# Repricing matmuls, scans and running sums in the order planner of a hybrid attention and mLSTM block

## The chip, the cores and the metric

The kernel runs on one core of one Trainium2 chip. The metric is the device time of one execution in microseconds, lower is better. The core has the engines PE (TensorE, matrix multiply), DVE (VectorE), ACT (ScalarE), POOL (GpSimd) and SP (SyncE, which here issues every DMA).

## The reference, cut to what matters

Two layers over 512 latent tokens and 256 context tokens, model width 1024, batch 1, all float32. One layer:

```
h  = rms_norm(x, norm_g) * (1 + scale) + shift          # scale, shift, gate = silu(c) @ w_mod + b_mod
aq,ak,av,az, bq,bk,bv,bo,bz,bg, cq,ck,cv,cz, gm = split(h @ w_in)
y_a = rms_norm(softmax_1 @ v - lam * softmax_2 @ v) * silu(az)      # A: 4 heads, 2-D rotary
y_b = sigmoid(bo) * rms_norm(mlstm forward + mlstm backward) * silu(bz)   # B: 4 heads, gates bg
y_c = neighbourhood_attention(cq, ck, cv, bias) * silu(cz)          # C: 8 heads
x   = x + gate * ((sum_n sigmoid(gm_n) * (y_n @ w_br_n)) @ w_out)
```

The last layer gives no context output; a final rms_norm ends the program. B's gate values are turned into prefix sums and prefix maxima along the 768 tokens before its heads can begin.

## The kernel before, in words

The work of a layer comes in stages: branch C, with B's gates worked out beside it (`branch_b_gates`), then branch A, branch B, the merge (`merge`: gate projections `gm` and branch projections, three rounds) and the output projection with the norm that leads to the next layer (`finish`). The long projections (`proj`, `proj_v`, tile `pj` in PSUM) are the main stream of PE. Each float32 product is three passes (high part by high part, high by low, low by high) over 128x128 weights with 512 or 256 moving columns; the split weights are the tile `wh`, whose low part is mostly made on POOL.

Heads run beside the main stream as generators. A head of C or A makes scores on PE (tile `gp`, a ring of three PSUM banks, or `sc`, one buffer), takes a row minimum on DVE, an exponential on ACT, normalises on DVE, transposes on PE and multiplies by the values on PE. B does the same with `tensor_tensor_reduce` (a product or sum with a running sum or minimum along the row) in the place of the softmax. `mod_rows` makes the modulation of later stages during the first layer's merge with 112 more instructions of that kind on tiles of 128x512. In the profile they stand as CUSTOM_DVE_ANT_0, followed by a DVE_READ_ACCUMULATOR2_ANT.

**The order is written by a planner.** While the program is built, the class `Sched` keeps a clock for each engine (T["P"] for PE, T["D"] for DVE and so on). Each instruction passes through `Sched.run` with a price in ns; it starts at the later of its engine's clock and the end of what it depends on plus a latency (LAT: 200 after PE, 130 after DVE, 150 after ACT). At every three or six matmuls of the main stream, `slot` looks at the side generators. One whose next step is to use PE goes on when its inputs are ready by PE's planned clock; one whose next step is on another engine may be 400 ns early (EARLY). Side work also pauses when DVE or ACT is planned more than 4000 ns ahead of PE (BACK), for `mod_rows` 1200 ns (REST). So the prices decide how many projection matmuls stand between a score and the transposes that need its softmax. The chip then runs each engine's list in the order written; the prices appear in no instruction.

Prices of DVE, ACT and POOL work are in `Timed.__getattr__` (all such instructions carry L345 in the profile, DMA issues L332), those of matmuls in `mm` (L381); transposes (L385) cost 109 ns. In `branch_b_gates` stand the only three scans of a layer (L1408, L1410, L1417), on 112x768:

```
V.tensor_tensor_scan(ib[:, ::-1], xf[:, ::-1], mk0[:, ::-1], 0.0, ALU.add, ALU.mult)
V.tensor_tensor_scan(pb, xf, mk1, 0.0, ALU.add, ALU.mult)
V.tensor_tensor_scan(mx, aa, aa, ib[:, 0:1], ALU.max, ALU.max)
```

Their generator runs beside the scores of the first head pair of C (`c_pair`). The row minimum of such a score is the tile `m` in the profile, its exponential writes `p` and gives the bank of `gp` back.

Of the kernel before, what the change touches and what calls it, by code (L numbers as in the profile page):

```python
# [12 lines left out]
F32 = mybir.dt.float32  # L13
# [284 lines left out]
def _space(ap):  # L298
    return getattr(ap, "space", None)


def _elems(ap):
    n = 1
    for s in list(ap.shape)[1:]:
        n *= int(s)
    return n


class Timed:
# [5 lines left out]
    def __getattr__(self, name):  # L315
        f = getattr(self.real, name)

        def call(*args, **kw):
            aps = [v for v in list(args) + list(kw.values()) if hasattr(v, "shape")]
            n = max(_elems(v) for v in aps)  # L320
            small = sum(1 for v in aps if _elems(v) == 1 and n > 1)
            psum = any(_space(v) == PSUM for v in aps[1:] + aps[:1])
            writes = [kw["out"] if "out" in kw else args[0]]
            if "accum_out" in kw:
                writes.append(kw["accum_out"])
            if name == "tensor_tensor_reduce":
                writes.append(args[-1])
            reads = [v for v in aps if not any(v is w for w in writes)]
            if name == "dma_start":
                out = kw["out"]  # L330
                self.sched.dma(int(out.shape[0]), int(out.shape[0]) * _elems(out) * 4, reads, writes)
                return f(*args, **kw)  # L332
            if self.eng == "D":
                one = len([v for v in aps if _elems(v) == n]) <= 2 and name in ("tensor_copy", "tensor_scalar", "memset")
                cost = n / (1.92 if one and not psum else 0.96) + 69.0 + 61.0 * small
                if name == "reciprocal":
                    cost = 69.0 + 8.0 * n
                if name == "tensor_tensor_reduce":
                    cost += 220.0
            elif self.eng == "A":  # L340
                cost = n * 0.8333 + (51.0 if psum else 93.0) + 93.0 * small
            else:
                cost = n * 2.15 + 130.0
            self.sched.run(self.eng, cost, reads, writes)
            return f(*args, **kw)  # L345
        return call
# [3 lines left out]
def kernel(ctx: ExitStack, tc: tile.TileContext, a: dict, out: bass.AP):  # L350
# [15 lines left out]
    S_ = Sched(bufs)  # L366
# [10 lines left out]

    def mm(o, l, r, start, stop, cost=None):
        n = _elems(o)
        S_.run("P", cost or (max(107.0, 0.4167 * n) + 2.0 if l.dtype != F32 else 1.67 * max(n, 128)), [l, r], [o])  # L380
        PE.matmul(o, l, r, start=start, stop=stop)  # L381

    def tr(o, i, idn):
# [197 lines left out]
    def mod_end(l, j, ps):  # L581

        yield from acq("t")
        rows = ring("t", [T])
        ACT.copy(out=rows[:, 0:512], in_=ps)
        rel("pj")
        yield "P"
        yield from acq("gp", "P")
        pt = ring("gp", [512])
        for b in range(4):  # L590
            mm(pt[:, 2 * b:2 * b + 2], rows[:, 128 * b:128 * b + 128], csel, True, True, 250.0)
        rel("t")
        yield
        pv = pt[:, 0:8].rearrange("p (b s) -> p b s", s=2)
        dst = modc[l][:, 4 * j:4 * j + 4, :]
        V.tensor_tensor(dst, pv,
                        prm[l][:, PRM_BMOD + 4 * j:PRM_BMOD + 4 * j + 4].unsqueeze(2).to_broadcast([128, 4, 2]), ALU.add)
        rel("gp")
        if j in (2, 3):
            k0 = 4 * (j - 2)  # L600
            V.scalar_tensor_tensor(gsc[l][:, k0:k0 + 4], dst, 1.0,
                                   prm[l][:, PRM_NG + k0:PRM_NG + k0 + 4].unsqueeze(2).to_broadcast([128, 4, 2]),
                                   ALU.add, ALU.mult)
        hit(modf[l][j])
# [70 lines left out]
    def mod_start():  # L675

        tags = ("pt", "pt", "v", "v", "pt", "pt")
        for u, (j, q) in enumerate(units):
            if q == 0:
                S_.need("pj")  # L680
                ps = ring("pj", [512])
            w = first_w[u]
            S_.until(lambda: S_.ready("P", [w], []) <= S_.T["P"])
            for i in range(2):
                k = 2 * q + i
                g = 32 * (k % 4)
                mm(ps[g:g + 32, :], cfz[:, k, :], w[:, 512 * i:512 * i + 512], k < 4, k >= 4, 430.0)
                S_.slot()
            if q == 3:
                S_.urgent(mod_end(0, j, ps))  # L690
            if u % 3 == 2 or u == 15:
                S_.free[tags[u // 3]].append(S_.T["P"] + S_.LAT["P"])
                if u in (2, 5):
                    fetch("pt", range(12, 15) if u == 2 else range(15, 16))
                    W.early = u == 2
        S_.free["cb"].append(S_.T["P"] + S_.LAT["P"])
# [31 lines left out]
    def norm_rows(acc, n, dg, aflag, res, nflag, tags):  # L728

        nt = n // 128  # L730
        yield from wait(aflag, KD, "P")
        ms, r = small(NT, "ms"), small(NT, "rr")
        for t0 in range(0, nt, 4):
            m = min(4, nt - t0)
            yield from acq("gp", "P")
            p = ring("gp", [512])
            for b in range(m):
                tr(p[:, 128 * b:128 * b + 128], acc[:, 128 * (t0 + b):128 * (t0 + b) + 128], ident)
            yield
            V.tensor_reduce(ms[:, t0:t0 + m], p[:, :128 * m].rearrange("p (b d) -> p b d", d=128), axis=AX.X, op=ALU.add)  # L740
            rel("gp")
        V.tensor_scalar(ms[:, :nt], ms[:, :nt], 1.0 / D, EPS, ALU.mult, ALU.add)
        yield from rsqrt_cols(r[:, :nt], ms[:, :nt], nt, "rt")
        for b in range(nt):
            V.tensor_scalar(dg[:, 128 * b:128 * b + 128], ident, r[:, b:b + 1], None, ALU.mult)
        for o in range(0, n, 512):
            w = min(512, n - o)
            yield from acq("gp", "P")
            p = ring("gp", [512])
            mm(p[:, :w], ones, dg[:, o:o + w], True, True)  # L750
            res.append(p[:, :w])
        hit(nflag)
        for t in tags:
            rel(t)
# [1159 lines left out]
```

## Time and profile before

| | |
|---|---|
| median of 3 runs | 1908.1 us (1907.88 to 1908.18) |
| the profiled execution's own time | 1906.09 us |
| its span, first to last instruction | 1904.3 us |
| PE busy | 1820.7 us, 96% |
| DVE busy | 1340.0 us, 70% |
| ACT busy | 858.7 us, 45% |
| POOL busy | 644.6 us, 34% |
| mean granted TensorE clock | 0.986 of full speed |

Busy time of PE is modelled from overlapping instructions, so it is the idle time and the start to start intervals that tell more. The profiled execution is 2.0 us below the median of the three runs and 1.8 us longer than its span.

### The profile page before, as it was taken

What the parts mean: (1) busy time and instruction counts of PE and PEld (TensorE: products, weight loads), DVE (VectorE), ACT (ScalarE), POOL (GpSimd) and SP (SyncE); (2) the same over time, 40 slices, a digit from 0 to 9 for tenths busy, and PEclk for the clock granted to TensorE, in tenths of its full rate; (3) what the DMA queues carried; (4) which work ended last, traced back from release to release, by engine and by line L of the source; (5) the groups of instructions that cost most, each with busy time, mean ns of one, the idle gap of its engine ahead of it and who ended that gap; (6) DMA issues with size and microseconds to landing.
All of it is one profiled execution on the core that took longest, in us unless ns stands there. A gap on an engine that the chain in (4) does not pass through costs nothing. (4 is left out here: it accounts for less than half of the span.)

```text
span 1904.3 us, 31909 instructions
## 1 busy us (share of the span) xinstructions
PE 1820.7 (96%) x11140; PEld 1604.8 (84%) x11140; DVE 1340.0 (70%) x3168; ACT 858.7 (45%) x1932; POOL 644.6 (34%) x563
## 2 busy tenths in 40 slices
PE   5999999999999999999999889999999999999996
PEld 2989998988899888888888779898888888788886
DVE  6676767888888775777763887766887787722336
ACT  4455555554555453222233444644555454432343
POOL 1332322221223322333335443432212323344455
PEclk9999999999999999999999989999999999999998
DMA  8333322222342453665546434333222424544444
GB/s 324 95 100 97 114 83 83 64 78 64 104 120 80 119 160 124 217 198 199 191 154 212 114 99 125 106 95 97 75 67 72 136 87 147 152 154 161 158 163 128
DMA packets 148479, 243.56 MB, mean 128 GB/s; under 512 B 18400, under 2 KB 52544, under 8 KB 148320
## 3 DMA queue, kind: packets, MB, share of 16 engines
q1 hardware_dynamic: 148320, 241.53, 40.5%
q8 instruction: 88, 1.44, 0.3%
q14 instruction: 71, 0.58, 0.1%
HBM read 199.45 MB, written 27.33 MB: 119 GB/s over the span
## 5 line engine op out<-in xcount | busy, mean ns | idle before, releaser
L381 PE MATMUL pj<-h,wh 128*128 128x512 f32 (+1 forms) x5664 | 1123.1, 352 | 2.7 <-ACT h L345 1.8
L381 PEld LDWEIGHTS pj<-h,wh 128*128 128x128 f32 x5664 | 900.9, 191 | 126.6 <-ACT h L345 2.0
L345 POOL TENSOR_TENSOR wh<-wr,wh 128x512 fp32r<-128x512 f32 (+1 forms) x409 | 563.7, 1385 | 1120.1 <-ACT wh L345 1066.3
L345 ACT CAST wh<-wr 128x512 fp32r<-128x512 f32 (+1 forms) x416 | 256.4, 621 | 385.5 <-PE pj L381 217.7
L381 PE MATMUL pj<-wh,h 128*128 128x256 f32 (+1 forms) x1728 | 236.2, 288 | 5.6 <-DVE h L345 3.7
L381 PEld LDWEIGHTS pj<-wh,h 128*128 128x128 f32 x1728 | 217.9, 191 | 9.2 <-DVE h L345 6.0
L345 DVE TENSOR_TENSOR pt<-gp,pt 128x512 fp32r<-128x512 f32 (+1 forms) x224 | 123.9, 573 | 87.8 <-ACT pt L345 86.5
L345 ACT CAST pt<-gp 128x512 fp32r<-128x512 f32 (+1 forms) x224 | 105.5, 496 | 152.1 <-PE gp L385 151.5
L381 PE MATMUL pj<-v,wh 128*128 128x512 f32 (+1 forms) x576 | 160.5, 358 | 0.0
L385 PE MATMUL gp<-ident,p 128*128 128x128 f32 x720 | 110.5, 276 | 17.6 <-DVE p L345 12.2
L381 PE MATMUL gp<-pt,v 128*128 128x256 f32 x864 | 117.2, 283 | 0.1
L381 PEld LDWEIGHTS pj<-v,wh 128*128 128x128 f32 x576 | 103.3, 189 | 15.7
L385 PEld LDWEIGHTS gp<-ident,p 128*128 128x128 f32 x720 | 84.1, 141 | 36.2 <-issue 17.9
L381 PEld LDWEIGHTS gp<-pt,v 128*128 128x128 f32 x864 | 110.5, 190 | 2.3 <-DVE pt L345 0.3
L345 ACT ACTIVATE t<-pj 128x512 f32<-128x512 f32 (+1 forms) x118 | 63.4, 537 | 102.4 <-PE pj L381 102.3
L381 PE MATMUL pj<-qk,wh 128*128 128x512 f32 (+1 forms) x288 | 103.1, 358 | 0.5 <-DVE qk L345 0.5
L345 DVE SCALAR_TENSOR_TENSOR t<-t,pj 128x512 f32<-128x512 f32 x66 | 38.4, 594 | 77.6 <-PE pj L381 77.6
L381 PE MATMUL sc<-qk 128*128 128x512 f32 (+1 forms) x360 | 83.1, 339 | 6.4 <-ACT p L345 4.8
L345 DVE TENSOR_REDUCE mna<-sc 128x1 f32<-128x768 f32 (+1 forms) x80 | 67.7, 846 | 30.3 <-PE sc L381 29.9
L345 ACT ACTIVATE p<-sc,mna 128x768 f32<-128x768 f32 (+1 forms) x80 | 65.5, 819 | 46.8 <-DVE mna L345 46.5
L345 DVE CUSTOM_DVE_ANT_0 sc<-cb,dt 128x512 f32<-128x512 f32 x56 | 56.6, 1011 | 36.2 <-DMA cb<-in_wmodr_dram 35.1
L345 DVE CUSTOM_DVE_ANT_0 sc<-cb,prm 128x512 f32<-128x512 f32 x56 | 62.6, 1118 | 25.3 <-DMA cb<-in_wmodr_dram 24.0
(145 smaller groups left out, 2089.8 us busy)
## 6 DMA issues: line engine op xcount, KB each, us to landing
wr<-in_wu_dram SPq DMA_DIRECT2D x296, 256.0 KB, 2.9
cb<-in_wmodr_dram SPq DMA_DIRECT2D x64, 256.0 KB, 3.8
wr<-in_wout_dram SPq DMA_DIRECT2D x64, 256.0 KB, 2.9
p<-afd SPq DMA_DIRECT2D x80, 192.0 KB, 4.1
wr<-in_wbr_dram SPq DMA_DIRECT2D x48, 256.0 KB, 2.9
q<-qk SPq DMA_DIRECT2D x160, 64.0 KB, 2.2
cb<-vd SPq DMA_DIRECT2D x32, 256.0 KB, 3.3
qk<-in_xT_dram SPq DMA_DIRECT2D x16, 384.0 KB, 6.3
```

The lines of the kernel that those rows point to most:

```text
L345: return f(*args, **kw)
L381: PE.matmul(o, l, r, start=start, stop=stop)
L385: PE.transpose(o, i, idn)
```

## The change

Three prices of the planner are altered; no operation is added or removed.

```
                 if name == "reciprocal":
                     cost = 69.0 + 8.0 * n
-                if name == "tensor_tensor_reduce":
-                    cost += 220.0
+                if name == "tensor_tensor_scan":
+                    cost = n / 0.48 + 430.0
...
-        S_.run("P", cost or (max(107.0, 0.4167 * n) + 2.0 if l.dtype != F32 else 1.67 * max(n, 128)), [l, r], [o])
+        S_.run("P", cost or (max(95.0, 0.4167 * n) + 13.5 if l.dtype != F32 else 1.67 * max(n, 128)), [l, r], [o])
```

A matmul of 512 columns goes from 215.3 to 226.9 ns, one of 256 from 109.0 to 120.2 ns. A scan of 768 goes from 869 (the third one, with a scalar operand, 930) to 2030 ns. A running sum goes down by 220 ns: in `mod_rows` from 944 to 724, in `c_pair` from 678 to 458 ns.

## Rows read from the trace of the kernel before

**Rows 1.** The page: busy us (share of the span) and instructions of each engine.

```profile
PE 1820.7 (96%) x11140; PEld 1604.8 (84%) x11140; DVE 1340.0 (70%) x3168; ACT 858.7 (45%) x1932; POOL 644.6 (34%) x563
```

**Rows 2.** Busy us by stretch: branches, first merge, branches; then granted clock, DMA.

```profile
150.00:750.00 600.00, 593.22 (x3940) 537.35 (x3939) 464.08 (x1281) 309.81 (x774) 161.58 (x168) 1.00 0.33 99
750.00:1050.00 300.00, 299.89 (x1680) 261.72 (x1679) 203.09 (x358) 87.48 (x157) 119.42 (x81) 1.00 0.58 193
1150.00:1700.00 550.00, 531.03 (x3262) 466.23 (x3263) 404.20 (x996) 274.22 (x643) 176.77 (x166) 0.99 0.36 106
```

**Rows 3.** Waits of PE, whole span: us in total, times, longest us.

```profile
PE gp L385 <- DVE p L345: 12.2, 12, 2.4
...
PE sc L381 <- ACT p L345: 4.8, 8, 1.6
```

**Rows 4.** Timeline of PE, first layer: start us, us, [idle before <-releaser].

```profile
91.84 0.40 PE L381 MATMUL gp<-qk 128*128 128x256 f32 x2
...
95.35 1.57 PE L381 MATMUL pj<-h,wh 128*128 128x512 f32 x9
99.73 0.80 PE L381 MATMUL gp<-qk 128*128 128x256 f32 x2 [2.81 <-ACT p L345]
```

**Rows 5.** Timeline of PE, second layer.

```profile
1121.80 0.40 PE L381 MATMUL gp<-qk 128*128 128x256 f32 x2
...
1125.68 1.58 PE L381 MATMUL pj<-h,wh 128*128 128x256 f32 x9
1134.16 0.79 PE L381 MATMUL gp<-qk 128*128 128x256 f32 x2 [6.91 <-ACT p L345]
```

**Rows 6.** Busy us by stretch (order of Rows 2), stretches of low granted clock.

```profile
99.10:105.90 6.80, 6.17 (x26) 5.77 (x27) 6.11 (x21) 4.62 (x13) 1.61 (x2) 0.50 0.28 68
1130.00:1140.20 10.20, 6.04 (x16) 4.98 (x17) 9.52 (x22) 4.40 (x11) 1.49 (x2) 0.50 0.32 92
```

**Rows 7.** Timeline of DVE: first layer's two sum scans, second layer's last scan.

```profile
86.45 3.41 DVE L345 TENSOR_TENSOR_SCAN pt<-pt,t 112x768 f32<-112x768 f32 x2
...
1129.03 1.82 DVE L345 TENSOR_TENSOR_SCAN v<-v,pt 112x768 f32<-112x768 f32 x1
...
1132.45 0.42 DVE L345 TENSOR_REDUCE m<-gp 128x1 f32<-128x256 f32 x1
```

**Rows 8.** Timeline of ACT, second layer.

```profile
1133.54 0.47 ACT L345 ACTIVATE p<-gp,m 128x256 f32<-128x256 f32 x1 [8.20 <-DVE m L345]
```

**Rows 9.** Timeline of PE: 512 columns back to back, and 256 columns.

```profile
1395.14 1.59 PE L381 MATMUL gp<-pt,v 128*128 128x256 f32 x12
1396.57 0.62 PE L381 MATMUL pj<-h,wh 128*128 128x512 f32 x2
...
1751.69 11.26 PE L381 MATMUL pj<-h,wh 128*128 128x512 f32 x48
1762.78 0.39 PE L381 MATMUL pj<-v,wh 128*128 128x512 f32 x1
```

**Rows 10.** Timeline of DVE and POOL in the first merge: running sums.

```profile
817.57 0.76 DVE L345 CUSTOM_DVE_ANT_0 sc<-cb,prm 128x512 f32<-128x512 f32 x1
817.91 3.27 POOL L345 TENSOR_TENSOR wh<-wr,wh 128x512 fp32r<-128x512 f32 x2 [6.41 <-ACT wh L345]
...
820.13 1.60 DVE L345 CUSTOM_DVE_ANT_0 sc<-cb,prm 128x512 f32<-128x512 f32 x1
821.66 0.14 DVE L345 DVE_READ_ACCUMULATOR2_ANT dt<- 128x1 f32 x1
```

**Rows 11.** Groups by shape, whole span: xcount, busy us, mean ns, idle before.

```profile
L345 DVE CUSTOM_DVE_ANT_0 sc<-cb,prm 128x512 f32<-128x512 f32 x56 | 62.6, 1118 | 25.3 <-DMA cb<-in_wmodr_dram 24.0
L345 DVE TENSOR_REDUCE mna<-sc 128x1 f32<-128x768 f32 x64 | 61.0, 953 | 23.0 <-PE sc L381 22.6
...
L345 DVE SCALAR_TENSOR_TENSOR p<-p,sma 128x768 f32<-128x768 f32 x32 | 38.9, 1217 | 1.1
...
L345 DVE CUSTOM_DVE_ANT_0 p<-gp,cb,m 128x256 f32<-128x256 f32 x64 | 31.0, 484 | 9.3
```

## The prediction, made before the change was run

> **What bounds the kernel now.** I read the page first. PE is busy for 96% of the span and no other engine for more than 70% [rows 1], so PE's list sets the end, and a new order can win or lose only what PE does not spend on streaming. The windows by stage say where that is: in the first merge PE idles 300 - 299.89 = 0.11 us, in the branch stages 6.78 us in the first layer and 18.97 us in the second, together 25.75 us [rows 2]. The list of PE's waits names what it waits for there, mostly transposes behind a softmax and scores behind an exponential that holds their PSUM buffer [rows 3]. The largest single wait of a branch, 6.9 us, is a score. The timelines find it and a smaller brother at the same place of each layer, beside B's gates: 2.81 us at 96.9 [rows 4] and 6.91 us at 1127.3 [rows 5]. The idle time is not all they cost: with each comes a stretch in which the granted clock is 0.50 of full speed, 1.2 instead of 2.4 GHz, 6.8 us in the first layer and 10.2 in the second [rows 6].
>
> **Why PE waits there.** The waiting score needs a bank of gp; the bank comes back with an exponential, which waited 8.20 us for the row minimum on DVE [rows 8]. That minimum, at 1132.45, stands in DVE's list behind the three scans and their neighbours [rows 7]. A sum scan takes 1.7 us in the first layer (3.41 for two) and the maximum scan 1.82 in the second [rows 7]; the planner counted 0.87 and 0.93. So the planner believed that DVE was free earlier than it is, and put too few matmuls ahead of the score.
>
> **The change, part by part.** No instruction changes its work; all effects are of order. The sum is made against the profiled execution (1906.09 us, 1.8 outside its span) and carried to the median, which is 2.0 us higher.
>
> Scans. The three go up by 1161, 1161 and 1100 ns, 3.42 us in all; by those rows about 2.6 were missing. All three lie ahead of the minimum in question, so planned PE has 3.42 us more to fill before the score that waits. Against this, the matmuls between the first score of the pair and the blocked one fill more planned time. They run for 95.35 + 1.57 - 91.84 = 5.1 us in the first layer [rows 4] and 5.5 in the second [rows 5]; at 6.6%, the mean rise of the price (below), that is 0.34 and 0.36 us. The softmax's own running minimum, 220 ns cheaper, takes off as much again. Net 2.85 us more real cover in either layer (3.42 - 0.35 - 0.22). The first wait, 2.81, goes, and I let its low clock go with it: half of 6.8 is 3.4, so 6.2 us. The second falls to 6.91 - 2.85 = 4.06, which is longer than the 2.81 that already came with a low clock, so I leave that in place: 2.8 us. Gain 9.0. Bounds: nothing, if the generators fall differently and the minimum stays behind everything else; and both waits with both low stretches, 2.81 + 3.4 + 6.91 + 3.0 = 16.1 (of the second stretch 1130.0 to 1140.2 only the 6.0 us after 1134.2 ran work, half of it lost).
>
> Matmuls. The 48 of 512 columns that start at 1751.69 end their turn at 1762.78: 231 ns each; the 12 of 256 from 1395.14 to 1396.57: 119 ns [rows 9]. The new prices, 226.9 and 120.2, are right to 2%; the old ones were 7 and 8% short. Being right is no gain in itself. PE's own work is the same; a price that was short put 5 to 10% more matmuls between a score and its dependents than the plan needed, a hidden reserve against DVE work that is also priced short. The reduce of 768 takes 953 ns against 930 counted, but the scaled difference after it 1217 against 930 [rows 11]. That reserve now goes. A softmax chain of A is 953 + 1217 and an exponential and a scaling between, an estimate of 4 us with hand-overs from those rows; the price rises by 5.4% at 512 columns and 10.3% at 256, and 6.6% over the mixture (an estimate from equal numbers of both by time, rounded down because transposes keep theirs), which is 0.26 us of cover. The two commonest waits of PE stand there 12 and 8 times [rows 3]. If each of the 20 grew by 0.26, 5.2 us; if as many again opened, 10.4. If one wait shields the next, as PE that stands still gives every other chain time, close to nothing. I take 3 us, rather more than half of the first, because chains overlap; bounds 0 and 10.4.
>
> Running sums. Where POOL does nothing, 512 columns take 0.76 us plus 0.14 to read the sum; beside POOL's subtraction of weights the same instruction takes 1.60 [rows 10]; the mean of the first half of them is 1118 ns [rows 11]. The plan had 944 and gets 724, so this edit moves away from the rows. In C, 484 ns plus a read stand against 678 before and 458 after, about as far off on the other side. In C and B it cuts 0.2 us more cover off a chain; I charge 1 us, between nothing and 20 x 0.22 = 4.4. In the merge I charge nothing: PE waits 0.11 us there [rows 2], and DVE has 300 - 203 = 97 us free, 24 of them spent ahead of the first half of these sums, waiting for the DMA that feeds them [rows 11]. What it costs without that cover is a rival below.
>
> The Trainium skill, page "SBUF — State Buffer", section "Who interferes with whom", says that DVE work with two SBUF inputs and GpSimd work that reads SBUF exclude each other for a whole instruction. The jump from 0.76 to 1.60 us agrees with it. By that rule the honest price of a running sum is about 850 ns alone and over 1.6 us beside POOL, never 724, and the sum would carry the second rival's charge instead of nothing.
>
> Sum: -9.0 + 3 + 1 = -5.0 us: 1901.1 for such an execution as the profiled one, 1903.1 against the median.
>
> **The rivals.** *The reserve eats the gain.* The scan waits shrink, but waits behind DVE grow by 6 to 12 us. For it: DVE is priced short in most chains; against it: 20 waits are few among thousands of matmuls. At 8 us lost, 1907, no change.
>
> *The reserve costs more than the scans give* (slower). Same place, branches A and B of the second layer, where DVE is fullest and 19 of the 25.75 us of idling lie [rows 2]. It decides when more is lost than the 9.0 us won and 3.8 besides: all of both upper bounds, 10.4 + 4.4 = 14.8, gives 1908.1 - 9.0 + 14.8 = 1913.9, and one new stretch of low clock like that of the first layer, 3.4 us, 1917.
>
> *Running sums jam the merge* (slower). Planned 24.6 us too fast in all (112 x 0.22), mod_rows is spread over less of the merge; DVE's list then holds a sum that waits for its DMA ahead of the operation that frees a projection bank. Two banks of 24 x 231 ns, 11 us, cover it; beyond that PE stands. At worst 13.6 us: 1908 - 5 + 13.6 = 1917. Against it: the 0.11 us of now.
>
> *The new price of scans does not reach the spot.* If the order around the gates stays as it is, only the charges are left: 1908 to 1912.
>
> **How the numbers follow.** Forecast, clearly faster, 46%: 1903.1, own range 1893 to 1904.2. Reserve eats the gain 23%; reserve wins 16%; running sums jam the merge 9%; scans miss the spot 6%, of which I give 4 to no change and 2 to slower. About 0.2%, 3.8 us, is what a measurement of this kernel can tell from no change. So faster 46%, same 27%, slower 27%. The range reaches down to 1893, where nearly all of the 16.1 us would come in, and up to 1916, which takes in all but the worst of the slower cases.
>
> **What would show it.** Right: the waits of 2.81 and 6.91 us on ACT p at the scores beside the gates fall under 0.5 and to about 4, DVE's list has the minimum m nearer to or ahead of the scans, and the low clock near 100 us is gone. Matmul intervals stay at 231 and 119. The charge would show as idle time in the two branch windows, 25.75 us now: up to 30 or so fits the sum, 35 and more means the reserve was worth more than I think, and under 25 that it was worth nothing. Idle time in the first merge above 1 us would show the running sums at work. Wrong altogether: new low-clock stretches in the branches, each of which takes about 3.4 us, at places that no term here names.

## The result and the profile after

| | before | after |
|---|---|---|
| median of 4 runs beside each other | 1907.99 us (1907.79 to 1908.18) | 1937.39 us (1933.77 to 1941.16) |
| profiled execution, its span | 1906.09, 1904.3 us | 1933.77, 1932.0 us |
| mean granted TensorE clock | 0.986 | 0.988 |

The changed kernel is slower: 1.0157 times the time before, interval 1.0145 to 1.017, 29.4 us by the medians and 27.7 by the two spans. That is outside the forecast's range (1893 to 1916), on its upper side.

The page, busy time by engine (beside [rows 1]):

```profile
PE 1829.1 (95%) x11140; PEld 1602.8 (83%) x11140; DVE 1336.6 (69%) x3165; ACT 859.1 (44%) x1932; POOL 640.5 (33%) x566
```

PE runs the same 11140 instructions and the clock is no lower, so no work was added and the clock gate did not take the time. The windows by stage say where PE stands still (order of [rows 2]: busy us of PE, PEld, DVE, ACT, POOL, then granted clock, DMA share, GB/s):

```profile
150.00:750.00 600.00, 581.76 (x3849) 522.64 (x3849) 460.25 (x1268) 304.66 (x763) 155.35 (x160) 1.00 0.32 96
750.00:1050.00 300.00, 297.19 (x1647) 257.99 (x1646) 188.52 (x344) 83.51 (x150) 106.11 (x75) 1.00 0.56 187
1150.00:1700.00 550.00, 522.49 (x3216) 455.84 (x3215) 421.81 (x1037) 277.64 (x656) 176.21 (x166) 0.99 0.35 104
```

PE idles 18.24 us in the first branch window instead of 6.78, 2.81 in the merge instead of 0.11, and 27.51 in the second branch window instead of 18.97: 22.7 us more in the three. Over the whole span idle time grows by 19.3 us and "busy" by 8.4 for the same instructions; busy time is modelled, so idle time does not show the whole loss. The windows are also fixed in time. The changed kernel reaches the second layer's gates some 24 us later, so that its second branch window holds 6.7 us of waits at the gates, which stood before 1150 us in the kernel before. A table further down counts idle time between the same matmuls instead. PE's waits over the whole span name the partners (total us, times, longest; beside [rows 3]):

```profile
PE gp L385 <- DVE p L345: 11.4, 15, 1.7
...
PE gp L385 <- DVE o L345: 10.4, 10, 3.1
PE gp L385 <- ACT p L345: 7.3, 3, 4.4
PE sc L381 <- ACT p L345: 6.6, 9, 1.6
PE sc L381 <- DVE den L345: 6.0, 7, 1.8
...
PE pj L381 <- DVE t L345: 2.8, 4, 0.9
```

Of the two waits that I had counted, one shrank (12.2 to 11.4) and one grew (4.8 to 6.6). Most of the new time lies where little or nothing stood before: transposes that wait for a finished head `o` of B, and scores that wait for B's `den`, had these rows in the kernel before:

```profile
PE sc L381 <- DVE den L345: 1.1, 3, 0.5
...
PE gp L385 <- DVE o L345: 0.8, 2, 0.5
```

The two places that the scans were to mend, in PE's timeline of the changed kernel (beside [rows 4] and [rows 5]):

```profile
96.79 2.30 PE L381 MATMUL pj<-h,wh 128*128 128x256 f32 x18
103.52 0.64 PE L385 MATMUL gp<-ident,pt 112*128 112x112 f32 x2 [4.43 <-ACT p L345]
...
1149.19 4.38 PE L381 MATMUL pj<-h,wh 128*128 128x256 f32 x24
1156.30 0.50 PE L381 MATMUL gp<-qk 128*128 128x256 f32 x2 [2.73 <-ACT p L345]
...
1170.19 0.66 PE L385 MATMUL gp<-ident,p 128*128 128x128 f32 x4 [1.78 <-ACT p L345]
```

and DVE's timeline ahead of the minima `m` that they hang on:

```profile
97.35 4.55 DVE L345 COPY pt<-v 48x768 f32<-48x768 f32 x7
101.82 0.41 DVE L345 TENSOR_REDUCE m<-gp 128x1 f32<-128x256 f32 x1
...
1152.61 2.08 DVE L345 TENSOR_TENSOR_SCAN v<-v,pt 112x768 f32<-112x768 f32 x1
1154.61 0.39 DVE L345 TENSOR_REDUCE m<-gp 128x1 f32<-128x256 f32 x1
```

In the second layer the minimum moved up right behind the scan and the wait fell from 6.91 to 2.73 us, but waits of 1.06 and 1.78 us for `p` and two shorter ones for `pt` follow it, which makes 6.7 us again. In the first layer it now stands behind seven copies, 4.55 us of DVE work that is no scan; the wait grew from 2.81 to 4.43 and sits at the gate transposes. The low clock shrank at the first place (3.4 us at 103.3 instead of 6.8 at 99.1); behind the second, 6.8 us remain of 10.2. In branch B of the second layer a stretch of 3.4 us is new, at the end of a wait of 3.10 us for `o`; one of 6.8 us at 1379.1 of the kernel before, in branch A, has no counterpart there (first three lines: after; last: before):

```profile
103.30:106.70 3.40, 3.18 (x9) 2.50 (x10) 3.09 (x12) 3.40 (x15) 2.16 (x3) 0.51 0.00 0
1171.70:1178.50 6.80, 5.79 (x25) 5.19 (x26) 6.55 (x18) 1.39 (x3) 3.04 (x3) 0.50 0.27 77
1574.50:1577.90 3.40, 2.85 (x9) 2.47 (x10) 2.95 (x10) 0.89 (x5) 0.00 (x0) 0.50 0.34 117
...
1379.10:1385.90 6.80, 5.92 (x16) 4.75 (x17) 3.89 (x15) 2.08 (x5) 0.00 (x0) 0.50 0.15 39
```

Matmuls run at the old intervals: 20 of 512 columns take 1755.46 - 1750.84 = 4.62 us, 231 ns each, as in [rows 9]:

```profile
1750.84 4.79 PE L381 MATMUL pj<-h,wh 128*128 128x512 f32 x20
1755.46 0.39 PE L381 MATMUL pj<-v,wh 128*128 128x512 f32 x1
```

### The profile page after: what moved, and what is told of

It is laid out like the page before. It is cut to its first block, busy times and chain, and to the rows that moved or that the text cites. A ratio compares the mean times of both kernels' runs of the same rounds, so it can differ in the third digit from the quotient of the medians.

```text
span 1932.0 us, 31924 instructions
## 1 busy us (share of the span) xinstructions
PE 1829.1 (95%) x11140; PEld 1602.8 (83%) x11140; DVE 1336.6 (69%) x3165; ACT 859.1 (44%) x1932; POOL 640.5 (33%) x566
## 4 chain that ended last, share of the span: by engine, by line
PE 62%; DVE 24%; DMA 5%; issue 4%; ACT 3%; POOL 1%; SPq 1%; DVEq 0%; ACTq 0%; POOLq 0%
PE pj L381 48%; PE gp L381 7%; DVE p L345 5%; PE gp L385 4%; DMA cb<-in_wmodr_dram 3%; PE sc L381 3%; DVE qk L345 3%; DVE t L345 3%; DVE sc L345 2%; DVE pt L345 2%; DVE ht L345 1%; DMA p<-afd 1%; DVE mna L345 1%; ACT p L345 1%; DVE h L345 1%
## 5 line engine op out<-in xcount | busy, mean ns | idle before, releaser
L381 PE MATMUL pj<-h,wh 128*128 128x512 f32 (+1 forms) x5664 | 1115.0, 351 | 4.9 <-ACT h L345 2.2
L381 PEld LDWEIGHTS pj<-h,wh 128*128 128x128 f32 x5664 | 900.0, 190 | 130.3 <-ACT h L345 2.6
L381 PE MATMUL pj<-wh,h 128*128 128x256 f32 (+1 forms) x1728 | 243.5, 291 | 5.6 <-DVE h L345 2.7
L381 PEld LDWEIGHTS pj<-wh,h 128*128 128x128 f32 x1728 | 222.7, 194 | 9.2 <-DVE h L345 4.4
L381 PE MATMUL pj<-v,wh 128*128 128x512 f32 (+1 forms) x576 | 160.1, 358 | 1.2 <-DVE t L345 1.2
L385 PE MATMUL gp<-ident,p 128*128 128x128 f32 x720 | 110.3, 277 | 18.6 <-DVE p L345 11.4
L381 PEld LDWEIGHTS pj<-v,wh 128*128 128x128 f32 x576 | 103.3, 189 | 18.1 <-DVE t L345 2.3
L381 PE MATMUL gp<-pt,v 128*128 128x256 f32 x864 | 117.2, 283 | 0.6 <-DVE pt L345 0.6
L385 PEld LDWEIGHTS gp<-ident,p 128*128 128x128 f32 x720 | 82.5, 141 | 39.7 <-issue 13.8
L381 PEld LDWEIGHTS gp<-pt,v 128*128 128x128 f32 x864 | 110.6, 190 | 2.8 <-DVE pt L345 0.8
L381 PE MATMUL pj<-qk,wh 128*128 128x512 f32 (+1 forms) x288 | 103.1, 358 | 0.4 <-DVE qk L345 0.4
L381 PE MATMUL sc<-qk 128*128 128x512 f32 (+1 forms) x360 | 83.8, 341 | 13.1 <-ACT p L345 6.6
L381 PEld LDWEIGHTS sc<-qk 128*128 128x128 f32 x360 | 57.3, 188 | 29.6 <-ACT p L345 12.6
L345 POOL TENSOR_TENSOR cb<-mskc,t 128x256 f32<-128x256 bf16 x64 | 51.5, 837 | 68.9 <-PE gp L381 35.7
```

The lines of the kernel that those rows point to most:

```text
L385: PE.transpose(o, i, idn)
```

## The experiments

Every kernel is the one before with the lines shown, so all differ in the written order alone; each was timed beside the kernel before on the same chip. "+20" means the difference of the two medians. Three theories were put to the test. *The reserve*: the old short matmul price and the long price of running sums gave DVE cover, and the change took it away. *Running sums*: they alone do the harm, by the merge. *The order*: the old order was a lucky one, and any other order loses some 20 us.

### The three parts alone and in pairs

Matmul price alone (m_only):

```
-        S_.run("P", cost or (max(107.0, 0.4167 * n) + 2.0 if ...
+        S_.run("P", cost or (max(95.0, 0.4167 * n) + 13.5 if ...
```

> Only the matmul price is new; scans and running sums keep the old prices. Theory 1 (the short matmul price was a reserve that covered DVE work which is also priced short): 15 to 30 us slower than before, with more idle time of PE in the branch stages. Theory 2 (the cheaper running sums cost the time): within 4 us of before. Theory 3 (the order of before is a lucky draw, any new order is slower by about the same): 15 to 30 us slower, like every other kernel here.

Scan price alone (s_only):

```
+                if name == "tensor_tensor_scan":
+                    cost = n / 0.48 + 430.0
```

> Only the price of the scans is new. Theories 1 and 2: 3 to 9 us faster than before, with the 6.91 us wait of the second layer's gates down to about 4 and nothing else touched, as six instructions are priced anew. Theory 3: 10 to 30 us slower, since the orders part at the first layer's gates and never meet again.

Running sums alone (r_only):

```
-                if name == "tensor_tensor_reduce":
-                    cost += 220.0
```

> Only the price of the running sums is new. Theory 1: within 5 us of before. Theory 2: 15 to 30 us slower, with waits of PE for DVE in the first merge and in branch B. Theory 3: 10 to 30 us slower, without such a place.

Pairs: matmuls and scans (m_s), scans and running sums (s_r), matmuls and running sums (m_r), the edits above put together.

> Matmul and scan prices new, running sums as before. Theory 1: 10 to 25 us slower, that is nearly all of the change, less the 3 to 9 us that the scans give. Theory 2: 0 to 9 us faster. Theory 3: 15 to 30 us slower.

> Scan and running sum prices new, matmuls as before. Theory 1: within 8 us of before. Theory 2: 10 to 25 us slower. Theory 3: 10 to 30 us slower.

> Matmul and running sum prices new, scans as before. Theory 1: 20 to 35 us slower, more than the whole change. Theory 2: 15 to 30 us slower, as the running sums alone. Theory 3: 15 to 30 us slower.

| kernel | median us | ratio to before, interval | difference |
|---|---|---|---|
| m_only | 1926.83 | 1.0106, 1.0086 to 1.0125 | +19.3 |
| s_only | 1900.64 | 0.996, 0.9946 to 0.9974 | -6.9 |
| r_only | 1920.47 | 1.0067, 1.0052 to 1.0082 | +12.9 |
| m_s | 1930.39 | 1.012, 1.0105 to 1.0135 | +22.8 |
| s_r | 1910.90 | 1.002, 1.0011 to 1.003 | +3.2 |
| m_r | 1949.22 | 1.0216, 1.0201 to 1.0231 | +41.5 |
| all three | 1937.39 | 1.0157, 1.0145 to 1.017 | +29.4 |

The single differences add up to 25.3, near the 29.4 of the whole. They are not independent: the matmul price costs 19.3 alone and 26 to 30 beside the others (22.8 + 6.9, 41.5 - 12.9, 29.4 - 3.2); the running sums cost 6.6 to 22.2 by what stands beside them (29.4 - 22.8, 41.5 - 19.3); the scans give 6.9 to 12.1 except beside the matmuls alone, where they cost 3.5. Two parts do harm, each by itself.

The scan price alone gives about as much as the forecast said of it. PE's timeline at the gates of s_only, both layers (L383 and L387 are L381 and L385 of before), and its windows:

```profile
108.92 0.50 PE L383 MATMUL gp<-qk 128*128 128x256 f32 x2 [0.82 <-ACT p L347]
...
1132.10 0.50 PE L383 MATMUL gp<-qk 128*128 128x256 f32 x2 [1.35 <-ACT p L347]
...
1136.96 0.50 PE L383 MATMUL gp<-qk 128*128 128x256 f32 x2 [1.55 <-ACT p L347]
...
1148.88 1.11 PE L387 MATMUL gp<-ident,p 128*128 128x128 f32 x4 [6.58 <-DVE pt L347]
```

```profile
85.00:150.00 65.00, 61.92 (x437) 56.71 (x436) 53.60 (x129) 30.12 (x78) 23.13 (x21) 1.00 0.37 106
...
150.00:750.00 600.00, 594.84 (x3950) 539.38 (x3949) 458.14 (x1286) 312.41 (x781) 165.18 (x170) 1.00 0.33 99
...
1150.00:1700.00 550.00, 533.80 (x3270) 471.11 (x3270) 398.83 (x999) 274.33 (x638) 177.62 (x166) 0.99 0.35 104
```

In the first layer the score that waited 2.81 us has no wait now (a later one has 0.82), and the granted clock is 1.00 where it was 0.95. Idle time there did not shrink, 3.08 us instead of 2.81, since a wait of 1.90 us for `pt` came in: what is gained is the clock. In the second layer the 6.91 became 1.35 and 1.55, but a new wait of 6.58 us behind them comes with a low clock of its own: transposes of `p` need a bank of `gp` that DVE empties into `pt`, in its list behind copies for the gates. The line of the kernel before for the first window:

```profile
85.00:150.00 65.00, 62.19 (x431) 58.17 (x431) 50.32 (x134) 29.81 (x79) 23.23 (x19) 0.95 0.37 104
```

Idle time of the two branch windows is 5.16 + 16.20 = 21.4 us.

The matmul price alone makes PE idle 20.79 + 24.67 = 45.5 us there (the whole change 45.75), of which 6.9 are the second layer's gate wait, late enough to fall into the window. It brings the `o` row, and at the first layer's gates a wait that was 2.81 us is 6.34:

```profile
150.00:750.00 600.00, 579.21 (x3837) 520.95 (x3835) 462.82 (x1259) 305.10 (x758) 153.58 (x158) 1.00 0.32 95
...
1150.00:1700.00 550.00, 525.33 (x3258) 460.85 (x3257) 424.29 (x1044) 279.97 (x660) 178.05 (x168) 0.99 0.35 106
```

```profile
PE gp L385 <- DVE o L345: 10.6, 12, 1.9
...
103.42 0.64 PE L385 MATMUL gp<-ident,pt 112*128 112x112 f32 x2 [6.34 <-ACT p L345]
```

What such a wait is made of is seen in the changed kernel, timelines of DVE, PE and POOL in the second layer's branch B:

```profile
1571.53 0.15 DVE L345 SCALAR_TENSOR_TENSOR hs<-ht,hs 128x2 f32<-128x2 f32 x1
1571.71 1.18 DVE L345 TENSOR_TENSOR ht<-hs 128x2 f32<-128x2 f32 x1
1572.92 1.23 DVE L345 SCALAR_TENSOR_TENSOR ht<-ht,hm 128x2 f32<-128x2 f32 x1
...
1574.38 0.61 DVE L345 TENSOR_SCALAR o<-gp,hs 128x128 f32<-128x128 f32 x2
...
1575.05 1.11 PE L385 MATMUL gp<-ident,o 128*128 128x128 f32 x4 [3.10 <-DVE o L345]
...
1571.60 2.54 POOL L345 TENSOR_TENSOR wh<-wr,wh 128x512 fp32r<-128x512 f32 x2 [1.01 <-ACT wh L345]
```

Two steps on 128x2 numbers take 1.2 us each while POOL subtracts weights and 0.15 when it does not, as the running sums of [rows 10] do. No price of the planner knows of that; here PE waits it out.

The running sums alone lose most clearly in a place that I had not named. In r_only PE idles 5 us near 360, in branch A, and the granted clock goes to 0.75. No running sum stands in DVE's list between 352 and 367 us, so their price must have acted there through the order of other work; how is not known:

```profile
355.00:365.00 10.00, 5.04 (x24) 3.17 (x22) 8.61 (x22) 5.00 (x15) 3.12 (x3) 0.75 0.40 108
```

In r_only's first merge PE idles 0.00 us (300 - 300.00), so there the merge theory falls. In the whole change the jam that it describes does occur, small (2.8 us in 4 waits, above). But m_only, with the old price of running sums, has it too (the first line below), while r_only and s_r have no such wait, so it needs the matmul price. Beside that price and 7% on DVE (below) the running sums do bring it back: none in m_s_dve107, 3.8 us in all_dve107. PE's waits in m_only, then PE's timeline and DVE's in the changed kernel:

```profile
PE pj L381 <- DVE t L345: 3.9, 3, 2.3
...
860.35 0.39 PE L381 MATMUL pj<-v,wh 128*128 128x256 f32 x1 [0.91 <-DVE t L345]
...
858.08 0.76 DVE L345 CUSTOM_DVE_ANT_0 sc<-cb,prm 128x512 f32<-128x512 f32 x1 [0.97 <-DMA cb<-in_wmodr_dram]
...
859.61 0.68 DVE L345 SCALAR_TENSOR_TENSOR t<-t,pj 128x512 f32<-128x512 f32 x1
```

A running sum waits 0.97 us for its DMA ahead of the operation that frees a bank of `pj`.

### Is it any new order, or a constant cover?

A matmul price 0.5 ns higher than before (nudge), and a constant cover of 300 ns on the whole change (all_margin300); MARGIN is the planner's own setting, 0 until now:

```
# nudge
-        ... (max(107.0, 0.4167 * n) + 2.0 if ...
+        ... (max(107.0, 0.4167 * n) + 2.5 if ...
# all_margin300: the whole change and
-    MARGIN = 0.0
+    MARGIN = 300.0
```

> The kernel before with each matmul counted half a nanosecond dearer (2.0 becomes 2.5 ns in its price, 0.2 to 0.5%), nothing else. It alters no price in a way that matters and is there to draw another order. Theory 1 and 2: within 4 us of before. Theory 3: 10 to 30 us slower.

> The whole change, and the planner's margin (the time that a side step on PE has to be ready ahead of PE's clock, so far 0) set to 300 ns: the reserve that the matmul price gave up is given back as a constant. Theory 1: at least half of the 29 us comes back, 0 to 15 us slower than before. Theory 2: the waits of the merge stay, but those of branch B shrink: 10 to 25 us slower. Theory 3: 15 to 30 us slower.

nudge: 1907.97 us, 0.9999 (0.999 to 1.0009), though 2862 of PE's 11140 instructions, counted in order, are not the ones that stand at the same place before. A different order costs nothing by itself, as far as one such order tells. all_margin300: 1932.90 us, 1.0128 (1.0113 to 1.0143), about 5 us better than the whole change: 0.3 us ahead of every step, more than the 0.26 of which I thought, does not bring the loss of the whole change back. With the matmul price alone a constant was not tried.

### DVE dearer by a factor

If it is the ratio of the two prices that counts, DVE should go up as matmuls did (5.4% and 10.3%). One line behind the DVE prices, in five kernels with the matmul price and one without it:

```
+                cost *= 1.07     # m_dve107: matmul price
+                cost *= 1.07     # m_s_dve107: matmul and scan price
+                cost *= 1.07     # all_dve107: whole change
+                cost *= 1.09     # all_dve109: whole change
+                cost *= 1.26     # all_dve126: whole change
+                cost *= 1.15     # s_dve115: scan price, old matmul price
```

> Only the matmul price new, and every price of DVE 1.07 times as high, so that the two engines stand to each other as before; ACT, POOL and all latencies stay. Ratio theory (what costs is how dear DVE is counted against PE, because DVE's list is dense and the shortfall adds up along a stage; a constant margin per step can't mend it): at least two thirds of the 20 us of the matmul price come back, within 7 us of before. Chain theory (each chain lost a constant piece of cover, and the margin of 300 ns was aimed at the wrong steps): 10 to 18 us slower than before, as 1.07 on DVE adds only some 0.2 us to a chain.

> The whole change, and every price of DVE 1.09 times as high; by the sums of the plan's own prices DVE then stands to PE nearly as it did before the change. Ratio theory: 0 to 8 us faster than before, as the price of the scans still helps. Chain theory: 15 to 25 us slower than before.

> The whole change, and every price of DVE 1.26 times as high, which brings the sum of its prices close to DVE's busy time in the trace, 1337 us against 1301. Ratio theory: the best of all, 5 to 20 us faster than before. Chain theory: 5 to 15 us slower than before. A third way it could go, if a plan that counts DVE too dear starts side work too late and the main stream runs out of buffers: slower than the one with 1.09.

> Only the scan price new, and every price of DVE 1.15 times as high, with the old matmul and running sum prices: more reserve than the kernel before has. Ratio theory: 10 to 20 us faster than before. Chain theory: 7 to 10 us faster, as the scan price alone. If the kernel before stands at the best ratio: slower than the scan price alone, 0 to 10 us slower than before.

> Matmul and scan prices new, DVE prices 1.07 times as high, running sums with their 220 ns. Broad ratio theory: the matmul price costs nothing once DVE is raised with it, so 2 to 8 us faster than before. Tiny step theory: 10 to 20 us slower, as 1.07 adds 5 ns to a step that is 130 short, and that 1.07 mended the matmul price alone was luck. Tuned point theory: within 6 us of before.

> The whole change with every DVE price 1.07 times as high; it differs from the run that came out 2 us slower than before only in the running sums. If the running sums cost where they stand: 10 to 22 us slower than before, the loss in branch B and in the first merge, none of note in C and A. If 1.09 was merely a bad draw: within 8 us of before.

| kernel | median us | ratio to before, interval | difference |
|---|---|---|---|
| m_dve107 | 1912.44 | 1.0023, 1.0012 to 1.0034 | +5.5 |
| m_s_dve107 | 1910.06 | 1.0011, 1.0001 to 1.0021 | +2.4 |
| all_dve107 | 1932.35 | 1.013, 1.0113 to 1.0147 | +24.5 |
| all_dve109 | 1931.57 | 1.0125, 1.011 to 1.0141 | +24.6 |
| all_dve126 | 1920.92 | 1.0068, 1.005 to 1.0085 | +13.9 |
| s_dve115 | 1927.42 | 1.0108, 1.0086 to 1.0131 | +20.4 |

7% on DVE takes 14 of the 19 us of the matmul price away, and 20 of the 23 of matmuls and scans. The windows of m_dve107 agree: 10.68 + 15.53 = 26.2 us idle in the branches, as before the change (25.75), and the `o` waits are back to 2.2 us from 10.6.

```profile
150.00:750.00 600.00, 589.32 (x3909) 530.47 (x3908) 466.36 (x1286) 309.94 (x775) 159.92 (x165) 1.00 0.32 96
...
1150.00:1700.00 550.00, 534.47 (x3280) 467.64 (x3279) 407.45 (x1021) 279.45 (x655) 178.85 (x168) 1.00 0.35 107
...
PE gp L386 <- DVE o L346: 2.2, 5, 0.7
```

So the matmul price did its harm through how it stood to DVE's prices. Whether it takes a factor on them, or a constant cover would do as well, these runs do not tell: on the whole change both were tried, and 7% (+24.5) and 300 ns (+25.2) give back about the same. With the running sums cheap, 7 and 9% help little (+24.5, +24.6 of +29.4): beside m_s_dve107 the running sums' price alone makes 22 us. 26% give back half (+13.9), but they also lift a running sum of `mod_rows` from 724 to 912 ns, near its old 944, so the two effects are mixed there.

And more is not better: s_dve115, where DVE is dearer against matmuls than in the kernel before, loses 20 us, and elsewhere. The larger part goes where the first layer's B runs into the merge. From 706.75 to 717.67 us PE's list has no projection left beside the last heads of B; PE idles 6.55 us of the first window below, and the granted clock falls. Some 7 us more go behind the first merge. Both windows of s_dve115, then those of the kernel before:

```profile
700.00:720.00 20.00, 13.45 (x72) 10.85 (x71) 16.66 (x53) 10.19 (x23) 4.36 (x8) 0.79 0.55 172
990.00:1040.00 50.00, 45.54 (x232) 38.14 (x231) 35.73 (x64) 16.82 (x34) 16.27 (x12) 0.93 0.62 211
```

```profile
700.00:720.00 20.00, 19.91 (x132) 17.82 (x131) 16.79 (x61) 9.24 (x25) 4.76 (x7) 1.00 0.31 102
990.00:1040.00 50.00, 49.89 (x227) 40.91 (x226) 22.29 (x33) 18.02 (x31) 22.09 (x17) 1.00 0.56 191
```

The last of `mod_rows`' running sums ends at 1054.1 us there, instead of 986.7 before and 984.9 in s_only, and DVE is busy 35.73 us in the second window instead of 22.29. A planner that takes DVE for full starts side work later (for `mod_rows`, REST), and what is left over then runs with no main work beside it; that this is the cause in both places was not tried by itself.

Time from one matmul of the main stream to another, the same ones in every kernel (the `pj` matmuls counted in order, first layer to second: numbers 64, 928, 1792, 2848 and 4160, then 4960, 5632, 6304 and 7072), as the difference to before in us, worked out from the starts in the traces:

| | C | A | B | merge | C, 2nd | A, 2nd | B, 2nd |
|---|---|---|---|---|---|---|---|
| whole change | +8.9 | -3.1 | +11.6 | +4.2 | +0.6 | -3.1 | +7.4 |
| m_only | +8.9 | -0.6 | +12.8 | +7.1 | +0.4 | -11.0 | +8.9 |
| s_only | -1.9 | -2.2 | -0.3 | +1.0 | -1.1 | -0.2 | +1.2 |
| r_only | +4.3 | +4.4 | +5.3 | +0.3 | +1.7 | +2.2 | +1.4 |
| m_dve107 | +4.9 | -1.2 | +0.9 | +4.5 | +1.8 | -4.0 | +3.2 |
| m_s_dve107 | +4.2 | -3.0 | +1.4 | +1.5 | -2.2 | -0.6 | +3.3 |
| all_dve107 | +3.4 | -8.0 | +21.4 | +6.7 | +1.6 | -0.8 | +1.1 |
| s_dve115 | +2.7 | +1.1 | +0.9 | +20.4 | +4.9 | -11.6 | -5.5 |
| nudge | -0.2 | +1.4 | +9.3 | -4.1 | -3.6 | +4.7 | -1.3 |

Single stages move by up to 9 us even in nudge, and cancel there; a stage is read from this table only where it is well beyond that. The running sums beside m_s_dve107 lose in the first layer's B (+20) and, less surely, in the merge (+5). PE's idle time between the same matmuls, in us:

| | C | A | B | merge | C, 2nd | A, 2nd | B, 2nd |
|---|---|---|---|---|---|---|---|
| before | 4.3 | 4.3 | 1.6 | 0.5 | 13.8 | 6.0 | 9.8 |
| whole change | 6.5 | 5.7 | 8.7 | 6.2 | 13.0 | 8.1 | 7.9 |
| m_only | 10.1 | 5.2 | 10.1 | 6.8 | 14.2 | 3.1 | 8.1 |
| s_only | 4.0 | 2.3 | 1.5 | 1.3 | 14.8 | 8.8 | 3.7 |
| r_only | 4.4 | 9.7 | 4.3 | 1.8 | 17.9 | 6.4 | 7.6 |
| m_dve107 | 5.3 | 4.7 | 2.7 | 3.2 | 13.8 | 5.2 | 7.3 |

So counted, A and B of both layers idle 21.7 us before and 30.4 in the whole change, and by both tables the matmul price's loss is the first layer's (28 us of time in its four stages): C, where its gates wait 6.34 us, B, and the merge with the way into it.

### Short steps, and how much a running sum should cost

A theory that came up on the way: what is short is the price of the many small steps, so a floor of 200 ns on every DVE price should give the cover back. And the price of running sums in steps (0 is s_r, 220 is s_only):

```
+                cost = max(cost, 200.0)   # all_floor200: whole change; s_floor200: scan price
# s_r110 and s_r330: scan price, and
-                    cost += 220.0
+                    cost += 110.0         # or 330.0
```

> The whole change, and no DVE instruction priced under 200 ns; the 128x2 steps of the head norms take 200 to 235 ns in the trace and are priced 71 to 85. Tiny step theory (the short matmul price covered these chains; without it the transposes of o wait for them): the waits of PE for DVE o fall from 10.4 us to 3 or less, branch B loses under 4 us in either layer instead of 11.6 and 7.4, and the whole is 5 to 15 us slower than before instead of 29. Broad ratio theory (all DVE prices are short and none of them alone carries it): 20 to 28 us slower. Tuned point theory (the planner's other constants fit the old prices and any large step from them costs, in either direction): 15 to 35 us slower.

> The scan price and the floor of 200 ns under DVE prices, matmuls and running sums as in the kernel before. Tiny step theory: 7 to 12 us faster than before. Broad ratio theory: 7 to 10 us faster. Tuned point theory: slower than the scan price alone, which gave 7 us.

> The scan price, and running sums with 110 ns on top instead of 220 or none, which is what they take in the trace without POOL beside them. If the running sum price works evenly: 1 to 3 us slower than the scan price alone, half of what the whole step costs beside it (10 us) or less. If it works by single accidents of order, as one stretch of the first layer's A suggests: anywhere from 8 us faster to 8 us slower than before.

> The scan price, and running sums with 330 ns on top instead of 220, away from the trace on the other side. If their price is a reserve, the more the better: 7 to 14 us faster than before. If the old prices sit between two losses: 0 to 10 us slower than the scan price alone, with the modulation rows of the first merge ending later than 987 us.

all_floor200: 1931.48 us, 1.012 (1.0104 to 1.0136), 6 better than the whole change. s_floor200: 1923.92, 1.008 (1.0064 to 1.0096), 23 worse than s_only. The theory falls: a floor that is closer to the rows helps little where cover is short and harms where it is not. s_r110: 1906.84, 1.0002 (0.9991 to 1.0012); s_r330: 1911.53, 1.0018 (1.0009 to 1.0028). Running sums at 0, 110, 220 and 330 ns more thus give 1910.9, 1906.8, 1900.6 and 1911.5 us: the old 220 is the best of the four, with a loss on both sides.

Scan price alone stays the best kernel found, 0.996 (0.9946 to 0.9974) of the time before.

## Why the prediction was wrong

*Scans: -9.0 forecast, -6.9 measured alone (bounds 0 to -16.1).* The size was right; the mechanism only in part, so that the size is luck to some degree. In s_only the first wait and its low clock go, as the working had it, but another wait takes the idle time up again. In the second layer the score's wait falls further than to 4, and the 6.58 us behind it, with a low clock, take most of that back. By the main stream the two C stages gain 1.9 and 1.1 us, where the working had 6.2 and 2.8; the profiled execution is 3.9 us shorter in all. In the whole change neither place gained: the first layer waits 4.43, because the minimum went behind copies that my working did not look at, and the second 6.7 in several pieces.

*Matmuls: +3 forecast, bounds 0 to 10.4; measured +19.3 alone and 26 to 30 beside the others.* This is the step that failed, by its size. The cause is the one that I named, a reserve that goes away: 7% on DVE's prices gives most of it back. I sized it as 0.26 us at each of the 20 waits that the kernel before had, and twice that at most. The waits that existed were the wrong list: chains with just enough cover do not appear in it, and those were the ones that opened (in m_only `o` from 0.8 to 10.6 us and `t` in the merge from nothing to 3.9; in the whole change `den` from 1.1 to 6.0 as well). At the first layer's gates, where I let 0.35 us of cover go, the wait in m_only is 6.34 us instead of 2.81. That a shorter cover also lets collisions of DVE with POOL through, each about 1 us where the working had 0.26, is seen in one wait above; what share of the 19 us it has was not measured.

*Running sums: +1 forecast, bounds 0 to 4.4; measured +12.9 alone, 3.2 + 6.9 = 10.1 beside the scans, 22 beside matmuls and scans with DVE at 7%.* The second failure, again a term too small. I looked at `mod_rows` and C, found the new price about as wrong as the old in C, and charged little. B's rows I had not looked at; by shape in the changed kernel (xcount, busy us, mean ns, idle):

```profile
L345 DVE CUSTOM_DVE_ANT_0 p<-sc,p 128x768 f32<-128x768 f32 x16 | 15.2, 952 | 1.9 <-ACT p L345 1.9
...
L345 DVE DVE_READ_ACCUMULATOR2_ANT den<- 128x1 f32 x80 | 6.6, 83 | 0.0
```

952 + 83 = 1035 ns stand against 768 / 0.96 + 69 + 220 = 1089 in the old plan and 869 in the new: B's were 5% long and are 16% short now. That fits the 20 us that all_dve107 loses in the first layer's B; it does not explain r_only, whose largest single loss is in A, where heads have no running sum. The mechanism of this term stays open. In the merge, which I charged nothing, the jam came and cost 2.8 us of 13.6 at worst, but it needed the matmul price (3.9 us in m_only, none in r_only).

*The rivals.* The one that came true is "the reserve costs more than the scans give", which had 16%. Its sign in the profile came: I wrote that 35 us and more of idle time in the two branch windows would mean a reserve worth more than I think, and they show 18.24 + 27.51 = 45.75. But 6.7 of these are the gates' waits that moved into the window, and between the same matmuls A and B gained only 8.7 us, so the sign was a rougher one than I took it for. It named the second layer, and the loss is mostly in the first (whole change: C +8.9, B +11.6). Its price was not right either: 1913.9 to 1917 against 1937. Of "new low-clock stretches", my sign for wrong altogether, there is one in the branches (3.4 us at 1574.5); the clock as a whole is not what cost the time, its mean being 0.988 against 0.986.

*The rule of the collisions.* In the traces of after, DVE's steps beside POOL's subtraction grow by about 1 us (the timelines above), as running sums did before [rows 10]. The rule that I set beside that row (the Trainium skill, page "SBUF — State Buffer", section "Who interferes with whom") agrees with both. What it spoke for, charging the running sums, was right as to the sign; but the merge, where I put its charge, has 2.8 us of waits for `t` in the whole change and none in r_only; most of what the running sums' price cost was lost elsewhere.

*What stays open.* Whether the matmul price needs a factor or a constant against it. Why the old prices lie at so good a point: matmuls 7% short, DVE short, running sums long in B and short in `mod_rows`. Dearer and cheaper DVE both lose, running sums lose on both sides of 220, and the planner's other settings (latencies, EARLY, BACK, REST) were not varied; they may have been settled together with the old prices, but nothing here shows it. Nor is it known why 7 to 9% on DVE, enough for the matmul price, does little once running sums are cheap.

## What to carry to other kernels

In a list scheduler, prices that agree better with the trace need not give a better plan: what counted here was how PE's price stood to DVE's, which decides how much main work stands between a step and its dependents, so a price that is corrected on one engine alone is a change of cover everywhere. Size such a change by all the chains that have just enough cover, not by the waits that the old trace shows. Try each price alone before putting three together: one of the three was worth 7 us, and the other two hid it. And compare idle time between the same instructions: a window fixed in time holds other work once a kernel is 20 us late.

## What the runs showed of the hardware

- Steps of DVE on 128x2 numbers take 0.15 us alone and 1.18 to 1.23 beside POOL's subtraction of weights: the collision costs these two-column steps about 1 us, more than the 0.84 us of a running sum of 512 (1.60 - 0.76, [rows 10]).
- A single wait of PE of 4.43 us came with 3.4 us of half clock, while two of 1.35 and 1.55 us, 4.9 us apart in s_only, came with none (granted clock 1.00 from 1125 to 1140); the 6.58 us wait behind them did (0.50 from 1146.7 to 1153.5).
